# Hybrid decoder step on one core: another table of issue orders, and the first norm's statistics in another PSUM bank

## Chip, cores and metric

The kernel runs on one core of one Trainium2 chip. Its time is the device time in microseconds of one execution. The engines are TensorE (PE, with its weight load PEld), VectorE (DVE), ScalarE (ACT), GpSimd (POOL) and SyncE (SP, which issues the loads and stores). Each takes its instructions strictly in its own program order; an instruction that has to wait holds up everything behind it on that engine.

## What is computed

One layer of a hybrid decoder for 1024 prompt positions and 8 sample sequences of 8 new positions, all in float32. Width 1024, 16 heads of 64 over 4 key and value heads, window 128, FFN width 2816 (two halves), convolution width 3.

```python
def layer(x, ...):
    h = rmsnorm(x, norm_mix)
    q, k, v, gu, gv, ga, gb = split_in(h @ w_in)
    o, nk, nv = attn_prompt(q, k, v, sinks)        # sample rows: attn_sample with cached keys
    vn = layernorm(gelu(gv), ln_g, ln_b)
    s = spatial_gating(gelu(gu), vn, ws, bs)
    merged = sigmoid(ga) * (o @ w_pa) + sigmoid(gb) * (s @ w_pb)
    x = x + merged @ w_out
    f, nconv = conv_ffn(rmsnorm(x, norm_ffn), w_up, conv_w, conv_b, w_down, conv_prev)
    return x + f, nk, nv, nconv, vn
...
y = rmsnorm(x, norm_final)
```

Attention is a softmax over a band of 128 keys with one learned sink per head; `spatial_gating` multiplies by a lower-triangular 128 x 128 matrix per channel group; `conv_ffn` is an up-projection, a causal convolution, `gelu(a) * b` and a down-projection. Outputs are the normed rows and the new caches.

## The kernel before

Activations lie transposed, features on the 128 partitions and tokens along the row. The tokens form two groups: group 0 with 576 columns (64 sample tokens and 512 of the prompt), group 1 with the other 512.

**Precision.** A float32 operand is split into a high part, rounded by a copy (`split` L40, or with a factor L44, both on ACT), and the rest, by a subtraction on DVE (L41). A product is three matmuls: high by high, high by low and low by high. In the code and the trace, `wh` and `wl` are the parts of a weight, `th` and `tl` of a combined activation, `hh` and `hl` of the normed input, `ph` and `pl` of attention's probabilities, `oh` and `ol` of its output.

**Products.** The input projection starts with `gv` from plain products (`mm_tok`, L533), with the weights as `w2h` and `w2l`. Most projections then go through `Chain.product` (L315): seven products of combined quarters in place of eight, in PSUM banks of the pool `psa` named "st", of which there are seven; some results are copied out to SBUF by ACT (`keep`, L294, tiles `k...`). The down-projection does the same in seven rounds (`mm_dn`, L1684; results "dn" added into `x` by L1694).

**The start.** SP loads blocks of `x`, the first block in two pieces (L595 and L602), the others whole (`load_x`, L354), between pieces of the first weights (L157). The products with gv use the input before its norm; the factor 1/rms follows as a scale when a result is read out of PSUM. `stats_tok` sums the squares of one group over the partitions by matmuls with a column of ones (L498), ACT takes the square root (L499, `rst`), DVE the reciprocal, and `gv_out` (L564) reads the gv banks with gelu and that scale.

**The gates.** Sigmoids of the gate columns (L852, tiles `z`) run on ACT beside the last chains of group 1. ACT also splits the sums that SP reads back from memory (`stg` from `sd`, L864, into `s`).

**Attention.** `attention` goes over pairs of (key head, block). For each pair PE makes scores (L1180), ACT exponentials (L1197), DVE the reciprocal of the sum and the scaling (L1199, L1200), PE transposes into `pt` (L1207), ACT and DVE split it to `ph` and `pl`, POOL masks both (L1217, `ch` and `cl`), and PE multiplies by the values (L1231) into the bank `po`, in four matmuls: ph, pl, ch, cl. ACT then copies one half of `po` out (L1236, `ot`), DVE adds the other (L1241, `of`, twice), and the sum is split into `oh` and `ol`. Meanwhile weights of coming products are split on ACT and DVE (`wh<-wraw`, `wl<-wraw,wh`).

**The end.** In the last round of the down-projection ACT squares finished pieces of `x` (L1703, `sq`) and DVE adds the squares up in `acc` (L1706); PE sums them over the partitions into a bank "fs" (L1739, L1729); ACT and DVE make 1/rms of it; `fin_mul` multiplies `x` by it (L1760), part of it on POOL, and SP stores `y`. The first token half is finished so while PE still works on the second.

**The order.** The program is written part by part, and then `issue_order` reorders each engine's whole list by the table `ORDER`: a string of numbers for each engine, each the number of places ahead, in what is left of the written order, from which the next instruction is taken (a dot is 0, "(n)" is n zeros).

```python
        for j in steps + [0] * (len(left) - len(steps)):
            now = left.pop(j)
            if last is not None:
                tc.add_manual_dep(now, last.name, ..., reason="issue order")
```

The order of each engine is thus fixed by the table; waits between engines follow from the data and from the reuse of tiles and banks.

Of the kernel before, what the change touches and what calls it, by code (L numbers as in the profile page):

```python
# [6 lines left out]
F32 = mybir.dt.float32  # L7
# [8 lines left out]
P = 128  # L16
# [18 lines left out]
def layer(tc, a):  # L35
# [11 lines left out]
    with ExitStack() as top:  # L47
# [295 lines left out]
        def pick(x, place, lo, hi):  # L343
# [3 lines left out]
        groups = [dict(g=0, n=576, off=0, soff=NS, base=192, mbase=448, blk0=0,  # L347
                       chunks=[(192, 0, 320), (512, 320, 576)],
                       toks=[("s", 0), *((i, NS + P * i) for i in range(4))]),
                  dict(g=1, n=512, off=576, soff=0, base=0, mbase=0, blk0=4,  # L350
                       chunks=[(0, 0, 512)], toks=[(4 + i, P * i) for i in range(4)])]
# [29 lines left out]
        with ExitStack() as ph1:  # L381
# [106 lines left out]
            psa = pso.enter_context(tc.tile_pool(name="psa", bufs=7, space=PSUM))  # L488

            def bank():  # L490
                return psa.tile([P, 512], F32, name="st")

            def stats_tok(g):

                acc = rsg[g]
                pt = bank()[:, :len(groups[g]["toks"])]
                for i, (_, lo) in enumerate(groups[g]["toks"]):
                    PE.matmul(pt[:, i:i + 1], acc[:, lo:lo + P], ones[:, 0:1], start=True, stop=True)  # L498
                S.activation(rstg[g], pt, AF.Sqrt, bias=eps, scale=1.0 / D)  # L499
                V.reciprocal(rstg[g], rstg[g])  # L500
# [120 lines left out]
            def first_out():  # L621
                stats_tok(0)
                for i in range(len(toks0)):
                    gv_out(0, i, 0, ps5[i])
# [58 lines left out]
            none = lambda: None  # L683
            jobs = [lambda: x_in(0)] + [x for kk in range(4) for x in (t0_job(kk), none)] + [t1_job(kk) for kk in range(4)]
            tokens(1, ("v", 1), lambda i, ps: v_out(1, i, ps), jobs, lambda: stats_tok(1))
            stats_all(1)
            wide["again"] = True
# [650 lines left out]
            for c in range(KD):  # L1338
                for at, go in enumerate(merge(1, c, operand(1))):
                    if at == 1:  # L1340
                        t, u = held.pop(c)
# [317 lines left out]
        with ExitStack() as ph3:  # L1659
# [109 lines left out]
            bank = [psd.tile([P, 512], F32, name="dn") for _ in range(6)]  # L1769
# [90 lines left out]
def issue_order(tc):  # L1860
# [8 lines left out]
    for name, text in ORDER.items():  # L1869
# [15 lines left out]
ORDER = {  # L1885
    "Pool": (
        "(34)mm(23)22..24..6(4)2..24..6(4)2..24..6(4)2..2(8)24..4..4..4..4..4..4..4..4..4..4..4..4(14)ff("
        "4)1..11..1...22(4)2213.2..1(5)6d3..2...3..2...63.b.2...3..2...63..2.8a..3..2..21(4)7.3..2...63.b"
        ".2...3..2...63.b.2...3..2...3.b4.52..2.1...3.4.2.8..3..2...63.b.2...3..2...63.b.2...3..2...6..53"
        "3.2.21"  # L1890
    ),
    "Activation": (
        "1.2(4)b..91.7.1.4..22.1...1(5)223..3(4)1..1.1..1.37..1.3..1..133..1(5)777cc.b..e1e.2.a3.33.22.4."
        ".39.1(5)66a.5..467(4)3.2.1.95a211..7...56(4)3..831.2...351..34(4)2..621.1.363..3.4.b.i4449.33.26"
        ".99.22.11.44..4c..4449e.f3.22.53.268(5)3.4.b.i4449.33.26.993.2.11.44..4c..4449e.f3.22.53.268(5)3"
        ".4.7.a4.39.8.3.2.5.4..9H49.7.d47.73.74.5.7...4.2.33.7b4.7132..62..225.4(4)2274ac2...85237221..2."
        "37.a47.127.6.2.5.4..48..49b7.3.4.5.6...3.4.7.a47.38.74...5.4..48..49b7.3.4.5.6...3.4.6.8d385.2.2"
        "44..2.1.5346246.44..9b.11.53241.3..1..311.y(4)433(5)5(5)2(5)y(5)O4(9)1.1.44(4)1.L(12)1.1.44(4)N1"
        ".44(4)1(9)Q(4)1.1.4(5)1.4(5)1.A(6)1(15)j1.44(5)1..q..H(6)4(5)T44(6)54(6)44(6)5S4(6)54(6)54(6)5P4"
        "(6)54(6)54M(6)54(6)54(6)5r4(6)54(6)54c(5)1...5.61..61.2515.51.123.22.24.15.151.14.51.152.142.24."  # L1900
        "13..45..7..1173..171.111.11(8)11...126.62.24.1..7..1..1.24..1(6)4..44..4.3.9.a.b3..a.922(4)5.4.."
        "9b..bd3...22...46...3.9.a.b3..a.92(5)5.4..9b..bd3...22...46...3.9.a.b3..a.92(5)5.4..9a..9a3...22"
        "421331..b1.3222..11.22..22.8.9bd3...2221571...3.9.a.b3..a.92211..5.4..9b..bd3...22...46...3.9.a."
        "b3..a.92(5)5.4..9b..bd3...22...46...3.9.9.93..7.622...22..51.5225266...5(4)1e.793..a.9322...5.4."
        ".9b..bd3...22...46...3.9.a.b3..a.92(5)5.4..9b..bd3...22...46...3.9.a.b3..a.92(5)5.4..9b..bd3...2"
        "2...46...3.7.7.7h..6..e1..124.341.1111.41525.1(5)1(7)1.1.1.1.1.1.1.1.1..1(4)KK[92]M.[90]L[89]N1M"
        "O[85]O.[83][83].[82][82].1(6)5(4)23.3.3.3.3.3.3.3.3.3.3.3.3.3.3.3.3.3.3.3(9)2j2i4.35e1466a.9.88."
        "71(8)11121..14l13514g62.466aaaaa.91.1.1...1(11)1...1.1...1"
    ),
    "DVE": (  # L1910
        "..nn2(6)91.7.1.4..2.1...1.1(5)23..3(4)1..1.1...26.1.31.2..2f.ee.dd1ck.jj.iii...777cc.bd.c.b2a.93"
        "88.87.62.222(4)2.2.33.22g.1(6)e.e.cccfic(4)8..66a(5)3.5.235f..3.e45..4..468.1.51..3.b.12.23.7.35"
        "..5.1.1...15..35[126]6[125]2[129][129]5.3[132][132]7.g[138].5[135]h.8(4)46(4)2449..26fi(4)66(4)4"
        "47..49.3h.6i.9(5)46(4)2449..26fi(4)66(4)447..47.3d.4e.51..24..254e55555yyyy.4w4v.24dg22.2.1..249"
        "6b.1..22.13c3.d..2..2496b.31..12138.a22..32546.3a.3b.2.13.6274a..47il..58...7.9.e.9.b..1b.ka.9.."
        "1h.7.8(4)6b8d(4)68hk(4)46..6.7.98.7..5.94.3..7.5..14233.32.1.14.2.124723.2.21(4)1(7)L1..227(4)4."
        "..11...11112.1(5)1111...2x(4)22(4)J..11.11..222(4)2N..11(4)2..11.11.252.1.11N.222(4)2..11(4)2R.."
        "11.11.2(4)2.1.2.11.1.2F..112.1.2..11(9)2.1.222...e.11...q(6)F(4)2(4)3332..151M33112.1.222..16154"
        "T1..262143...1..3227..1..332N..151.22..1.4.22O..262.43...1..322..1..332t..262.43(5)4.227g.1.11(4"
        ")1b.22d.11...2.b..34f.2.9.3..714.73.5.b4.66.b.44..587..3..5.1.4.1.3.5...2.2413..31.131.2.3.7..d."  # L1920
        ".35.1..14..2..11.3(8)32(4)u.y(5)25.16.244..3(5)12.2.24143561454223.3...1..114.1.2.41112221.1.1.."
        "2262c5c.ag.9i..7...46(4)2g5g..ddim...aa(4)8..6.f..6..aa.f9i..7...46(4)2g5g..ddim...aa(4)8..6.f.."
        "6..aa.f9i..7...46(4)2g5g..ddhj...aa...8.7..4.4.2.7..5..3.2(5)11.4.e3.cc1h.aaah(4)8..6.f..6..aa.f"
        "9i...6..46(4)2g5g..ddim...aa(4)8..6.f..6..aa.f9i..7...46(4)2g5g..ddim...aa(4)8..6.f..6..aa.e9f.."
        "7...45..3...1b.bag.9..7.6..6.5.2.14.a3ca..7.6ae.5.6(4)25fg..ddim...aa(4)8..6.f..6..aa.f9i..7...4"
        "6(4)2g5g..ddim...aa(4)8..6.f..6..aa.f9i..7...46(4)2g5g..ddim...aa(4)8..6.b..6..66.55...b2a..1133"
        ".33(7)1322.1..7..4..2.1.1(8)1(4)54..1(8)1..11.11.11.11.11...11.a.8..1.4.[75]3(4)11.[67][69].[68]"
        "[70]..11.[65](7)7(6)2b.b.b8..1..6(5)23.3.3.3.3.3.b.b.b8b(5)3(4)23.3.3.3(9)88.7...77.12...11.1..3"
        "..11..11(10)21311111...88(4)4a4...a..118.111.11.111...41.1.2(4)12...2.21.1"
    ),  # L1930
    "SP": (
        "..1(21)6789(4)7...3.2.a.ach(10)7.e.d.3d.c.1o(5)99.aa...948..625(4)33.23f.e..11..1..23(15)271(5)1"
        "(4)11.3..1.OOT1S...TTVV61.1.2..1.13.2..61.1.2..1.13.2..5615...2..232622.12.1212tt.vy..2.424...1."
        ".1.3..62.1.2..464.1.1.4191312.411.21.21c.1512125.1..11.11.1a1411.141...589..1264.11...2231...246"
        "6214..2fs1z1(25)1c.1i6p31...2.m2.63(4)2t.2.s63(4)2.m2.fd.aaab.ib.mf(9)eb(5)79.792(4)3a.d7.6g.j7."
        "1.j1(4)1321(13)1(5)1.2...2.1.21113.52544..4..244..244..54.3.5731.8c4..1133.8K..I2...22..56..y333"
        "..1112.111l11(7)22222211..1.445221.111444455.4477...4455.4477...455.55883(4)3344...44.44...44.66"
        "...1551.44...44.44...44.44...44.99...6(6)1...111f12..3333333..1.98(7)111(40)122.111(5)1.a.9999.8"
        "88l.lmn.no(24)1.1.1...1...1.1.1.1.1.1.1.1"
    ),  # L1940
    "PE": (
        "(26)1(14)1(14)112(3646)8888888(13)999(22)4444(6)9999(405)3(139)3333(31)44(113)4444444(60)4444444"
# [97 lines left out]
```

## Time and profile before

| | before |
|---|---|
| median of three runs | 1503.83 us (1502.03 to 1504.26) |
| profiled execution | 1502.3 us |
| its span in the profile | 1500.6 us |
| mean granted clock of TensorE | 0.998 |
| PE busy | 1487.9 us, 99% |
| DVE, ACT, POOL busy | 79%, 57%, 18% |
| instructions | 30059 |

A row of the timeline reads: start in microseconds from the start of the span, duration, engine, line of the kernel, operation, output and inputs by name, shapes, how many in a row; in brackets the idle time of the engine ahead of it and what ended that. A row of the list of waits reads: engine, tile and line that waited, what it waited for, microseconds in total, how often, the longest. A row of windows gives the stretch, its length, then busy time and number of instructions of PE, weight load, DVE, ACT and POOL, the granted clock, the busy share of the DMA engines and the GB/s moved.

### The profile page before, as it was taken

How to read it: one execution, taken by the hardware profiler on the slowest of the kernel's cores; microseconds unless marked ns; L12 is line 12 of the kernel's file. 1: busy time of each engine (PE TensorE's matmuls, PEld its weight loads, DVE VectorE, ACT ScalarE, POOL GpSimd, SP SyncE). 2: the span in 40 equal slices, each digit the busy share in tenths (PEclk: the TensorE clock that was granted, in tenths of full speed). 3: DMA queues.
4: the chain of work that ended last, by engine and by line, in shares of the span. 5: the costliest groups of instructions: out<-in, count | busy, mean ns of one | idle time of the engine just before them, and what ended most of it. 6: DMA issues, size and time to landing. Idle time of an engine off the chain costs nothing.

```text
span 1500.6 us, 30059 instructions
## 1 busy us (share of the span) xinstructions
PE 1487.9 (99%) x11508; PEld 1451.1 (97%) x11508; DVE 1180.2 (79%) x1886; ACT 856.2 (57%) x1790; POOL 272.4 (18%) x375
## 2 busy tenths in 40 slices
PE   9999999999999999999999999999999999999997
PEld 9999999999998989988989999999999999999997
DVE  7798877655576887979578988898898888785686
ACT  7557676654465776764444555555555556363463
POOL 0001000010030222320234322332142222000002
PEclk9999999999999999999999999999999999999999
DMA  7687546864669757448988433332232216983453
GB/s 258 220 282 249 177 164 224 251 217 158 230 232 306 219 171 236 148 159 303 335 293 283 131 112 119 120 121 109 103 140 101 104 63 231 335 298 98 113 172 142
DMA packets 134431, 289.88 MB, mean 193 GB/s; under 512 B 15760, under 2 KB 36560, under 8 KB 134288
## 3 DMA queue, kind: packets, MB, share of 16 engines
q1 hardware_dynamic: 134144, 287.96, 56.7%
q8 instruction: 90, 1.47, 0.4%
q14 instruction: 53, 0.43, 0.1%
q10 hardware_dynamic: 144, 0.01, 0.0%
HBM read 198.97 MB, written 90.92 MB: 193 GB/s over the span
## 4 chain that ended last, share of the span: by engine, by line
PE 93%; DMA 2%; DVE 2%; ACT 1%; issue 1%; POOL 1%; SPq 0%; POOLq 0%; ACTq 0%; DVEq 0%
PE st L315 50%; PE mm L240 16%; PE dn L1684 14%; PE st L533 7%; PE po L1231 2%; PE sc L1180 2%; PE pt L1207 1%; DMA wl<-upd 1%; PE mx L814 1%; DMA sg1d<-z 0%; DMA x1d<-x1g 0%; DMA x<-xt 0%; POOL cl L1217 0%; DVE pl L41 0%; ACT wh L40 0%
## 5 line engine op out<-in xcount | busy, mean ns | idle before, releaser
L315 PE MATMUL st<-t,wh 128*128 128x288 f32 x2128 | 427.6, 294 | 0.0
L315 PEld LDWEIGHTS st<-t,wh 128*128 128x128 f32 x2128 | 335.5, 188 | 0.1
L315 PE MATMUL st<-t,wl 128*128 128x288 f32 x1064 | 311.9, 293 | 0.0
L315 PE MATMUL st<-th,wh 128*128 128x256 f32 x1064 | 295.2, 278 | 0.6 <-ACT k L294 0.6
L315 PE MATMUL st<-tl,wh 128*128 128x256 f32 x1064 | 294.4, 277 | 0.0
L315 PE MATMUL st<-th,wl 128*128 128x256 f32 x1064 | 294.1, 276 | 0.0
L315 PEld LDWEIGHTS st<-th,wh 128*128 128x128 f32 x1064 | 199.8, 188 | 1.4 <-ACT k L294 1.2
L315 PEld LDWEIGHTS st<-t,wl 128*128 128x128 f32 x1064 | 199.7, 188 | 0.3 <-DMA wl<-upd 0.3
L315 PEld LDWEIGHTS st<-th,wl 128*128 128x128 f32 x1064 | 199.9, 188 | 0.0
L315 PEld LDWEIGHTS st<-tl,wh 128*128 128x128 f32 x1064 | 199.8, 188 | 0.0
L1684 PE MATMUL dn<-th,wh 128*128 128x288 f32 (+1 forms) x616 | 176.7, 287 | 0.1
L1684 PE MATMUL dn<-tl,wh 128*128 128x288 f32 (+1 forms) x616 | 176.5, 286 | 0.0
L1684 PE MATMUL dn<-th,wl 128*128 128x288 f32 (+1 forms) x616 | 175.0, 284 | 0.0
L40 ACT CAST wh<-wraw 128x512 fp32r<-128x512 f32 (+2 forms) x188 | 129.4, 700 | 79.6 <-PE st L315 27.2
L41 DVE TENSOR_TENSOR wl<-wraw,wh 128x512 fp32r<-128x512 f32 (+2 forms) x188 | 148.2, 801 | 31.2 <-ACT wh L40 29.1
L40 ACT CAST wh<-ws 128x512 fp32r<-128x512 f32 x168 | 102.5, 621 | 90.9 <-PE st L315 55.1
L41 DVE TENSOR_TENSOR wl<-ws,wh 128x512 fp32r<-128x512 f32 x168 | 117.6, 711 | 40.9 <-ACT wh L40 40.1
L1684 PEld LDWEIGHTS dn<-th,wh 128*128 128x128 f32 x616 | 115.6, 188 | 0.4 <-ACT zb L341 0.3
L1684 PEld LDWEIGHTS dn<-th,wl 128*128 128x128 f32 x616 | 115.9, 188 | 0.1
L1684 PEld LDWEIGHTS dn<-tl,wh 128*128 128x128 f32 x616 | 115.7, 188 | 0.1
L533 PE MATMUL st<-w2h,hh 128*128 128x256 f32 x288 | 80.2, 279 | 1.0 <-ACT hh L44 0.7
L533 PE MATMUL st<-w2h,hl 128*128 128x256 f32 x288 | 79.8, 278 | 0.0
(281 smaller groups left out, 3181.2 us busy)
## 6 DMA issues: line engine op xcount, KB each, us to landing
wraw<-wt SPq DMA_DIRECT2D x137, 512.0 KB
traw<-td SPq DMA_DIRECT2D x77, 272.0 KB
td<-za SPq DMA_DIRECT2D x22, 544.0 KB
q<-qd SPq DMA_DIRECT2D x16, 512.0 KB
upd<-hl SPq DMA_DIRECT2D x14, 512.0 KB
td<-t SPq DMA_DIRECT2D x11, 544.0 KB
wpart<-wt SPq DMA_DIRECT2D x22, 256.0 KB
qd<-q SPq DMA_DIRECT2D x8, 576.0 KB
```

Of the source, the lines that this page charges most:

```text
L40: S.copy(hi, src)
L41: V.tensor_sub(lo, src, hi.bitcast(F32))
L240: PE.matmul(ps[:, lo:lo + c1 - c0], u[:, k, :], v[:, c0:c1], start=(k == 0 and i == 0), stop=(k == nk - 1 and i == 2))
L315: PE.matmul(ps, u[:, kk, :], v, start=first and kk + i == 0, stop=kk == 3 and i == 2, skip_group_check=True)
L533: PE.matmul(ps, u[:, lo:lo + P], v[:, k, :], start=k + i == 0, stop=k == KD - 1 and i == 2)
L814: PE.matmul(ps[:, P * i:P * i + P], vn[:, i], late["wst"][:, c, :], start=True, stop=True)
L1180: PE.matmul(ps[:, h, o0:256], q, kst[kv][:, e, k0:cur + P], start=e == 0, stop=e == 1)
L1207: PE.transpose(pt[:, h * P:h * P + P], s[:, h, 0:P], ident)
L1231: PE.matmul(po, v[:, kv, :], t, start=e == 0, stop=last)
L1684: PE.matmul(place(m, e), u[:, m, :], v[:, lo:hi], start=new and i + k == 0 and (e == 0 or m % 2 == 0), stop=i == NU - 1 and k == 2, skip_g ...
```

## The change

Two edits. The column that receives the statistics of the first norm comes from the bank "mx" of the same pool instead of one of the seven banks "st":

```diff
             def stats_tok(g):
 
                 acc = rsg[g]
-                pt = bank()[:, :len(groups[g]["toks"])]
+                pt = psa.tile([P, 512], F32, name="mx", bufs=1)[:, :len(groups[g]["toks"])]
                 for i, (_, lo) in enumerate(groups[g]["toks"]):
```

And the strings of `ORDER` for Pool, Activation, DVE and SP are others (PE's stays). The first line of Activation's:

```diff
-        "1.2(4)b..91.7.1.4..22.1...1(5)223..3(4)1..1.1..1.37..1.3..1..133..1(5)777cc.b..e1e.2.a3.33.22.4."
+        "1.2(4)b..91.7.1.4..22.1(9)223..3(4)1..1.1..1.37..1.3..1..133..1(5)777cc.b..e1e.2.a3.33.22.4..39."
```

66 instructions stand some places earlier or later; none is added or removed. Other moves than those below: in SP, L602 now stands ahead of L354 at the start, and loads near 425 us and near the down-projection's start are exchanged; in ACT, a copy (L294) and two sigmoids (L852) stand ahead of splits of `stg` near 425 and 438 us, in the chains of q and k a copy (L294) and casts of q (L834) are exchanged, and in group 0's attention `ot` stands ahead of `ph` three times; in DVE, splits and evacuations of the up-projection between 800 and 850 us are exchanged; in POOL, one run of instructions.

ACT at the first norm, where `rst` is the root of the statistics, `w2h` the high part of a weight and `gv` the gelu of the first results:

```order
 L615 ACTIVATE x_267<-x_267 128x576
-L40 CAST w2h<-wraw 128x1024
+L40 CAST w2h<-wraw 128x1024 x2
 L499 ACT_TABLE_LOAD
-L499 ACTIVATE rst_228<-st,c_eps 128x5
-L40 CAST w2h<-wraw 128x1024
+L499 ACTIVATE rst_228<-mx,c_eps 128x5
 L564 ACT_TABLE_LOAD
 L564 ACTIVATE gv<-st,rst_228 128x256 x4
```

The second split of a weight now stands ahead of the statistics' table load instead of behind its result, and the statistics come from "mx".

DVE in group 1's attention, about 603 to 610 us, before: `nm` is a maximum of scores, `dn` a sum of exponentials, `pl` the low part of the probabilities, `wl` that of a coming weight, `of` and `ol` the output of attention and its low part:

```order
L1241 TENSOR_TENSOR of<-po,ot 64x256
L1194 TENSOR_REDUCE nm<-s 128x4
L1241 TENSOR_TENSOR of<-po,ot 64x256
L41 TENSOR_TENSOR pl<-pt,ph 128x512
L41 TENSOR_TENSOR wl<-wraw,wh 128x1024
L1199 RECIPROCAL dn<-dn 128x4
L41 TENSOR_TENSOR ol_7921<-of,oh_7920 128x2x128
```

And the same place now:

```order
L1241 TENSOR_TENSOR of<-po,ot 64x256
L1194 TENSOR_REDUCE nm<-s 128x4
L41 TENSOR_TENSOR pl<-pt,ph 128x512
L1241 TENSOR_TENSOR of<-po,ot 64x256
L41 TENSOR_TENSOR ol_7921<-of,oh_7920 128x2x128
L41 TENSOR_TENSOR wl<-wraw,wh 128x1024
L1199 RECIPROCAL dn<-dn 128x4
```

The split `pl` stands ahead of the second evacuation, and `of` and `ol` stand between it and the weight's split. In ACT the cast of the same weight stands behind `ph` at this place.

DVE at the end of the down-projection, from about 1478 us: `x_17062` is the second token half, `x_16747` the first, `acc` the sums of squares:

```order
 L1694 TENSOR_TENSOR x_17062<-x_17062,dn 128x288
-L1760 TENSOR_TENSOR x_16747<-x_16747,fs 128x576
+L1706 TENSOR_TENSOR acc_16746<-acc_16746,sq 128x288
+L1694 TENSOR_TENSOR x_17062<-x_17062,dn 128x288
+L1760 TENSOR_TENSOR x_16747<-x_16747,fs 128x576 x2
 L1694 TENSOR_TENSOR x_17062<-x_17062,dn 128x288
 L1706 TENSOR_TENSOR acc_16746<-acc_16746,sq 128x288
-L1760 TENSOR_TENSOR x_16747<-x_16747,fs 128x576
-L1706 TENSOR_TENSOR acc_16746<-acc_16746,sq 128x288
-L1694 TENSOR_TENSOR x_17062<-x_17062,dn 128x288
-L1760 TENSOR_TENSOR x_16747<-x_16747,fs 128x512
```

All three additions into `acc` now stand ahead of the last two scalings of the first half; before, the third addition had three scalings ahead of it.

More of the change, by code (lines that the diff above doesn't have):

```diff
@@ L1887 @@
         "(34)mm(23)22..24..6(4)2..24..6(4)2..24..6(4)2..2(8)24..4..4..4..4..4..4..4..4..4..4..4..4(14)ff("
-        "4)1..11..1...22(4)2213.2..1(5)6d3..2...3..2...63.b.2...3..2...63..2.8a..3..2..21(4)7.3..2...63.b"
-        ".2...3..2...63.b.2...3..2...3.b4.52..2.1...3.4.2.8..3..2...63.b.2...3..2...63.b.2...3..2...6..53"
-        "3.2.21"
+        "4)1..11.2(4)22(4)2213.2..1(5)6d3..2...3..2...63.b.2...3..2...63..2.8a..3..2..21(4)7.3..2...63.b."
+        "2...3..2...63.b.2...3..2...3.b4.52..2.1...3.4.2.8..3..2...63.b.2...3..2...63.b.2...3..2...6..533"
@@ L1891 @@
+        ".2.21"
     ),
     "Activation": (
-        "1.2(4)b..91.7.1.4..22.1...1(5)223..3(4)1..1.1..1.37..1.3..1..133..1(5)777cc.b..e1e.2.a3.33.22.4."
[L1894 to L1907, printed above, removed]
@@ L1908 @@
-        "71(8)11121..14l13514g62.466aaaaa.91.1.1...1(11)1...1.1...1"
+        "1.2(4)b..91.7.1.4..22.1(9)223..3(4)1..1.1..1.37..1.3..1..133..1(5)777cc.b..e1e.2.a3.33.22.4..39."
+        "1(5)66a.5..467(4)3.2.1.95a211..7...56(4)3..831.2...351..34(4)2..621.1.363..3.4.b.i4449.333.6.99("
+        "7)44..4c..4449e.f3.22.53.268(5)3.4.b.i4449.33.26.993.2.11.44..4c..4449e.f3.22.53.268(5)3.4.7.a4."
+        "39.8.3.2.5.4..9H49.7.d47.73.74.5.7...4.2.33.7b4.7132..62..225.4(4)2274ac2...85237221..2.37.a47.1"
@@ new lines @@
+        "27.6.2.5.4..48..49b7.3.4.5.6...3.4.7.a47.38.74...5.4..48..49b7.3.4.5.6...3.4.6.86c37.2.244..2.1."
+        "534624..433.9b.11.53241.3..1..311.y(4)433(5)5(5)2(5)y(5)O4(9)1.1.44(4)1.L(4)1(7)1.1.44(4)N1.44(4"
+        ")1(5)1...Q(4)1.1.4(5)1.4(5)1.A(6)1(5)1(9)j1.44(5)1..q..H(6)4(5)T44(6)54(4)1.44(6)54R(6)54(6)54(6"
+        ")Q54(6)54(6)54M(6)54(6)54(6)s44..1...54(6)54c(5)1...5.61..61.2515.51.123.22.24.15.151.14.51.152."
+        "142.24.13..45..7..1173..171.111.11(8)11...126.62.24.1..7..1(4)24..1(6)4..44...33.9.a.b3..a.9222."
@@ new lines @@
+        "..5.4..9b..bd3...22...46...3.9.a.b3..a.92(5)5.4..9b..bd3...22...46...3.9.a.b3..a.92(5)5.4..9a..9"
+        "a3...22421331..b1.3222..11.22..22.8.9bd3...2221571...3.9.a.b3..a.92211..5.4..9b..bd3...22...46.."
+        ".3.9.a.b3..a.92(5)5.4..9b..bd3...22...46...3.9.9.93..7.622...22..51.5225266...5(4)1e.793..a.9322"
+        "...5.4..9b..bd3...22...46...3.9.a.b3..a.92(5)5.4..9b..bd3...22...46...3.9.a.b3..a.92(5)5.4..9b.."
+        "bd3...22...46...3.7.7.7h..6.f.1..124.341.1111.41525.1(5)1(7)1.1.1.1.1.1.1.1.1..1(4)KK[92]M.[90]L"
@@ L1909 @@
+        "[89]N1MO[85]O.[83][83].[82][82].1(6)5(4)23.3.3.3.3.3.3.3.3.3.3.3.3.3.3.3.3.3.3.3(9)2j2i4.35e1466"
+        "a.9.88.71(8)11121..14l13514g62.466aaaaa.91.1.1...1(11)1...1.1...1"
     ),
@@ L1912 @@
         "88.87.62.222(4)2.2.33.22g.1(6)e.e.cccfic(4)8..66a(5)3.5.235f..3.e45..4..468.1.51..3.b.12.23.7.35"
-        "..5.1.1...15..35[126]6[125]2[129][129]5.3[132][132]7.g[138].5[135]h.8(4)46(4)2449..26fi(4)66(4)4"
+        "..5.1.1...15..35[126]6[125]2[129][129]5.37[131].g.[138]5[136].g8[124](4)46(4)2449..26fi(4)66(4)4"
         "47..49.3h.6i.9(5)46(4)2449..26fi(4)66(4)447..47.3d.4e.51..24..254e55555yyyy.4w4v.24dg22.2.1..249"
@@ L1916 @@
         "1h.7.8(4)6b8d(4)68hk(4)46..6.7.98.7..5.94.3..7.5..14233.32.1.14.2.124723.2.21(4)1(7)L1..227(4)4."
[L1917 to L1929, printed above, removed]
+        "..11...11112.1(5)1111...2x(4)22(4)J..11.11..222..1.2N..11(4)2..11.11.252.1.11N3312121.2..11(4)2R"
@@ new lines @@
+        "..11.11.2(4)2.1.2.11.1.2F..112.1.2.22(10)2.1.222...e.11...q(6)F(4)2(4)3332..151M33112.1333...161"
+        "44.S..262133...1..3227..1..322N..151.32..1.4.22O..262.43...11433...1..222t..262.43(5)4.227g.1.11"
+        "(4)1b.22d.11...2.b..34f.2.9.3..714.73.5.b4.6.5b.44..587..3..5.1.4.1.3.5...2.2413..31.131.2.3.7.."
+        "d..633.1.14..2..11.3.2...11.32..w222.x(4)25.16.244..3(5)12.2.241435616542451221.1..11424163.2444"
+        "313...1..2262c5c.ag.9i..7...46(4)2g5g..ddim...aa(4)8..6.f..6..aa.f9i..7...46(4)2g5g..ddim...aa(4"
@@ new lines @@
+        ")8..6.f..6..aa.f9i..7...46(4)2g5g..ddhj...aa...8.7..4.4.2.7..5..3.2(5)11.4.e3.cc1h.aaah(4)8..6.f"
+        "..6..aa.f9i...6..46(4)2g5g..ddim...aa(4)8..6.f..6..aa.f9i..7...46(4)2g5g..ddim...aa(4)8..6.f..6."
+        ".aa.e9f..7...45..3...1b.bag.9..7.6..6.5.2.14.a3ca..7.6ae.5.6(4)25fg..ddim...aa(4)8..6.f..6..aa.f"
+        "9i..7...46(4)2g5g..ddim...aa(4)8..6.f..6..aa.f9i..7...46(4)2g5g..ddim...aa(4)8..6.b..6..66.55..."
+        "b2a..1133.3.2(6)1322.1..7..4..2.1.1(8)1(4)513.1(8)1..11.11.11.11.11...11.a.8..1.4.[75]3(4)11.[67"
@@ L1930 @@
+        "][69].[68][70]..11.[65](7)7(6)2b.b.b8..1..6(5)23.3.3.3.3.3.b.b.b8b(5)3(4)23.3.3.3(9)88.7...77.12"
+        "...11.1..3..11..11(10)21311111...88(4)4a4...a..118.111.11.111...41.1.2(5)2..3.32..1"
     ),
     "SP": (
-        "..1(21)6789(4)7...3.2.a.ach(10)7.e.d.3d.c.1o(5)99.aa...948..625(4)33.23f.e..11..1..23(15)271(5)1"
-        "(4)11.3..1.OOT1S...TTVV61.1.2..1.13.2..61.1.2..1.13.2..5615...2..232622.12.1212tt.vy..2.424...1."
-        ".1.3..62.1.2..464.1.1.4191312.411.21.21c.1512125.1..11.11.1a1411.141...589..1264.11...2231...246"
@@ L1935 @@
[L1935 to L1939, printed above, removed]
+        "(24)6789(4)7...3.2.a.ach(10)7.e.d.3d.c.1o(5)99.aa...948..625(4)33.23f.e..11..1..23(15)21.5(4)1(4"
@@ new lines @@
+        ")11.3..1.OOT1S...TTVV61.1.2..1.13.2..61.1.2..1.13.2..5615...2..232622.12.1212tt.vy..2.424...1..1"
+        ".3..62.1.2..464.1.1.4191312.411.21.21c.1512125.1..11.11.1a1411.141...589.7.4124..241.231...24662"
+        "14..2fs1z1(25)1c.1i6p31...2.m2.63(4)2t.2.s63(4)2.m2.fd.aaab.ib.mf(9)eb(5)79.792(4)3a.d7.6g.j7.1."
+        "j1(4)1321(13)1(5)1.2...2.1.21113.52544..4..244..244..54.3.5731.8c4..1133.8K..I2...22..56..y333.."
+        "1112.111l11(7)22222211..1.445221.111444455.4477...4455.4477...455.55883(4)3344...44.44...44.66.."
@@ L1940 @@
+        ".1551.44...44.44...44.44...44.99...6(6)1...111f12..3333333..1.988...11122(41)122.111(5)1.a.9999."
+        "888l.lmn.no(24)1.1.1...1...1.1.1.1.1.1.1.1"
     ),
```

## The prediction

> **What bounds the kernel.** I read the page first, then PE's list of waits, then the timeline at each place where that list or PE's spacing shows a hole. Of the page, the busy times and the chain that ended last:
>
> ```profile
> PE 1487.9 (99%) x11508; PEld 1451.1 (97%) x11508; DVE 1180.2 (79%) x1886; ACT 856.2 (57%) x1790; POOL 272.4 (18%) x375
> PE 93%; DMA 2%; DVE 2%; ACT 1%; issue 1%; POOL 1%; SPq 0%; POOLq 0%; ACTq 0%; DVEq 0%
> ```
>
> PE sets the end. The change takes no matmul away, so it can win only where PE stands still. PE's list of waits (microseconds in total, times, longest) names such places:
>
> ```profile
> PE fs L1739 <- DVE acc L1706: 1.5, 1, 1.5
> PE po L1231 <- POOL cl L1217: 1.0, 3, 0.4
> PE st L533 <- ACT hh L44: 0.7, 1, 0.7
> PE st L315 <- ACT k L294: 0.6, 2, 0.4
> PE po L1231 <- ACT s L1197: 0.4, 1, 0.4
> PE st L533 <- ACT rst L499: 0.4, 1, 0.4
> PE po L1123 <- DVE of L1144: 0.3, 1, 0.3
> ```
>
> Moved instructions stand right ahead of all of these but the last. The list counts only recorded idle time; I use the larger number, the distance from one matmul's start to the next less the usual distance, since a matmul's recorded length overlaps its neighbour's.
>
> **Part A, the load of x at 2 us.** SP issues the second half of the first block (L602) behind the whole second block (L354), and the ACT split waits for a load:
>
> ```profile
> 1.74 0.43 SPq L354 DMA_DIRECT2D x<-xt  x1
> 2.21 0.43 SPq L602 DMA_DIRECT2D x<-xt  x1
> 6.43 1.18 ACT L44 ACTIVATE hh<-x,c_gains 128x256 fp32r<-128x256 f32 x2 [1.78 <-DMA x<-xt]
> 6.04 0.28 PE L533 MATMUL st<-w2h,hl 128*128 128x256 f32 x1
> 6.99 0.38 PE L533 MATMUL st<-w2h,hh 128*128 128x256 f32 x1 [0.68 <-ACT hh L44]
> ```
>
> PE stands 6.99 − 6.04 = 0.95 instead of 0.11 (two matmuls of 256 columns in the quoted stretches below start 0.11 apart), so 0.84 at most. The two issues swap. One place earlier in SP is 2.21 − 1.74 = 0.47, and I take that the load lands earlier by as much: 0.45. From 0 (the split is then held by the next load) to 0.84.
>
> **Part B, the first norm at 24 us.** The statistics now lie in the bank "mx", so the next product takes its own "st" bank and no longer the one that ACT still reads:
>
> ```profile
> 23.46 1.17 PE L498 MATMUL st<-c_ones,rs 128*128 128x1 f32 x10
> 24.98 0.39 PE L533 MATMUL st<-w2h,hh 128*128 128x256 f32 x1 [0.36 <-ACT rst L499]
> 24.67 0.27 ACT L499 ACTIVATE rst<-st,c_eps 128x5 f32<-128x5 f32 x1 [1.49 <-PE st L498]
> 24.83 1.04 ACT L40 CAST w2h<-wraw 128x1024 fp32r<-128x1024 f32 x1
> ```
>
> The product starts at 24.98, just when rst ends (24.67 + 0.27 = 24.94); the ten matmuls end at 24.63. So 0.35 of idle time and 0.11 of a slow first matmul (0.39 against 0.28): 0.45, from 0 to that. The same bank change would only move the wait on by one product if the gelu's four instructions came late; ACT's cast of 1.04 now stands ahead of the first table load, in the 1.49 of idle time, so table and gelu come about 1.04 earlier. That is what keeps this term from being given back.
>
> **Part C, the last products of group 1.** ACT copies a partial product (L294) that the next product's accumulation needs; behind it stood other work:
>
> ```profile
> 428.25 0.28 PE L315 MATMUL st<-th,wl 128*128 128x256 f32 x1
> 428.94 0.38 PE L315 MATMUL st<-th,wh 128*128 128x256 f32 x1 [0.42 <-ACT k L294]
> 424.89 0.63 ACT L852 ACTIVATE z<-z 128x512 f32<-128x512 f32 x1
> 425.43 0.39 ACT L341 ACTIVATE z<-st 128x288 f32<-128x288 f32 x1
> 440.11 0.28 PE L315 MATMUL st<-th,wl 128*128 128x256 f32 x1
> 440.58 0.38 PE L315 MATMUL st<-th,wh 128*128 128x256 f32 x1 [0.19 <-ACT k L294]
> 437.75 0.67 ACT L40 CAST s<-stg 128x576 fp32r<-128x576 f32 x1 [1.19 <-DMA stg<-sd]
> ```
>
> The holes are 0.69 − 0.11 = 0.58 and 0.47 − 0.11 = 0.36. In the first, a sigmoid (L852, 425.43 − 424.89 = 0.54 of ACT's time) is moved ahead of a cast that waits for a load anyway, so the copy comes 0.54 earlier. In the second, a copy and a sigmoid move into the 1.19 in which ACT waited for a load. Sum 0.54 + 0.36 = 0.9, from 0 to that. SP issues the loads behind those casts (stg from sd) earlier, and two weight and mask loads later; I cost those at nothing.
>
> **Part D, attention of group 1.** Three times PE waits for the masked low part of the probabilities (POOL, cl), and DVE is what holds POOL:
>
> ```profile
> 609.01 0.40 PE L1231 MATMUL po<-ch,dvst 128*128 128x512 f32 x1
> 609.77 0.50 PE L1231 MATMUL po<-cl,dvst 128*128 128x512 f32 x1 [0.37 <-POOL cl L1217]
> 606.71 0.59 ACT L40 CAST ph<-pt 128x512 fp32r<-128x512 f32 x1
> 607.40 0.69 DVE L41 TENSOR_TENSOR pl<-pt,ph 128x512 fp32r<-128x512 f32 x1 [0.17 <-ACT ph L40]
> 608.01 1.22 DVE L41 TENSOR_TENSOR wl<-wraw,wh 128x1024 fp32r<-128x1024 f32 x1
> 608.16 1.56 POOL L1217 TENSOR_SCALAR_AFFINE_SELECT cl<-pl 128x512 fp32r<-128x512 f32 x1 [0.16 <-DVE pl L41]
> 613.71 0.64 POOL L1217 TENSOR_SCALAR_AFFINE_SELECT cl<-pl 128x512 fp32r<-128x512 f32 x1 [0.29 <-DVE pl L41]
> 605.64 1.05 ACT L40 CAST wh<-wraw 128x1024 fp32r<-128x1024 f32 x1
> ```
>
> Where DVE's long weight split (1.22) follows pl at once, POOL's instruction takes 1.56; where not, 0.64. The list counts 1.0 for the three, one of them here, 0.37; and the matmul behind the wait took 0.50 where the one ahead took 0.40, so 0.1 more each: 1.3. With the 0.4 of the list's row on s (L1197), where an evacuation moves ahead of a split, 1.7. Now ACT makes ph ahead of the weight cast (1.05 earlier at the first place), pl stands ahead of one evacuation, and an evacuation stands between pl and the weight split. The first and the last of these each exceed the wait, so I take all of it, 1.7, and 0 as the other end. What speaks against full value is how full DVE is there (engine columns PE, weight load, DVE, ACT, POOL):
>
> ```profile
> 600.00:650.00 50.00, 48.62 (x345) 45.28 (x344) 47.32 (x89) 39.67 (x125) 17.89 (x30) 1.00 0.41 134
> ```
>
> DVE is busy for 47.32 of 50. What is late next is an evacuation (of), now behind a pl of 0.69, and by the list one has been late only once, for 0.3, in the sample group's part (L1123). In group 0's attention ot goes ahead of ph three times; I cost that at nothing, since the list shows no such wait above 0.3.
>
> **Part E, the end of the down-projection.** PE's longest hole is the wait for the sums of squares of one token half:
>
> ```profile
> 1482.95 0.28 PE L1684 MATMUL dn<-th,wh 128*128 128x256 f32 x1
> 1484.72 0.75 PE L1739 MATMUL fs<-acc,c_ones 128*128 128x288 f32 x2 [1.49 <-DVE acc L1706]
> 1479.54 0.82 DVE L1706 TENSOR_TENSOR acc<-acc,sq 128x288 f32<-128x288 f32 x1
> 1480.94 1.02 DVE L1706 TENSOR_TENSOR acc<-acc,sq 128x288 f32<-128x288 f32 x1
> 1483.22 1.45 DVE L1706 TENSOR_TENSOR acc<-acc,sq 128x288 f32<-128x288 f32 x1
> 1478.61 5.74 POOL L1760 TENSOR_TENSOR x<-x,rb 128x576 f32<-128x576 f32 x4 [219.17 <-ACT rb L1753]
> ```
>
> The hole is 1.77, less 0.11: 1.66. Three sums stand among four scalings (L1760); now two scalings follow the second addition, and the third and fourth come last. POOL's four instructions of 5.74 / 4 = 1.43 end at about 1480.05, 1481.48, 1482.91 and 1484.35, and the sums end 0.31, 0.48 and 0.32 behind three of these: while POOL works, a sum of two SBUF tiles gets through only between two of its instructions. Worked in the new order, the first sum ends before POOL begins, the second at about 1481.95 and the third, without a scaling ahead of it, behind the boundary at 1482.91, at about 1483.35. PE would then start at 1483.40 instead of 1484.72: 1.3. From 0 (the third sum misses its gap) to 1.66. The Trainium skill, "SBUF — State Buffer", sections "SBUF: two separate sides" and "Who interferes with whom", states this as an exclusive lock: a VectorE instruction with two inputs in SBUF and a GpSimd instruction that reads SBUF share a port pair, and the one that starts first keeps it for its whole length. By that rule POOL's fourth instruction, if it starts first, keeps the third sum out until 1484.35, and this part brings nothing; the trace's 1.56 against 0.64, and its sums' ends, agree with a lock.
>
> **Small moves at nothing.** DVE's reordered splits and evacuations around 800 to 850 us, SP's order near 425 and 1260 us, and POOL's small change each pass instructions nobody waits for in the list. For the chance that one such move opens a wait I take off one wait of the smallest size listed, 0.3.
>
> **Sum.** 0.45 + 0.45 + 0.9 + 1.7 + 1.3 − 0.3 = 4.5. The profiled execution took 1502.3 (span 1500.6 and 1.7 around it), so 1497.8 for such an execution. The median of the runs, 1503.83, lies 1.5 above it; the forecast for the median is 1503.83 − 4.5 = 1499.3. With every upper end and no new wait the gain is 0.84 + 0.45 + 0.9 + 1.7 + 1.66 = 5.55, so 1498.3; and the three runs of before lie between 1502.03 and 1504.26, 1.1 to either side of their middle, so 1497.2 at the lowest.
>
> **Rivals.**
>
> *Locked at the end.* The third sum misses its gap, Part E brings 0: gain 3.2, 1500.6. For it: 0.4 us decide, and 1483.22 + 1.45 shows how it looks when the gap is missed. Against: without the scaling the sum is queued before the gap. Chance 0.12.
>
> *Covered.* In Parts C and D the queues are full and the moved work only exchanges one wait for another: 0.45 + 0.45 + 1.3 − 0.3 = 1.9, 1501.9, no measurable change. For it: DVE's 47.32 of 50, and ACT's 39.67. Against: the waiting instruction has spare time behind it where the list is silent. That the bank change does nothing belongs here too: if "mx" were not free at 24 us the product would wait as before, 0.45 of this sum. Chance 0.21.
>
> *The evacuation becomes late, slower.* In attention, ot moves behind wh at two places (1.05 each, and 0.59 of ph at one) and of moves behind pl at five (0.69 each): 2 × 1.05 + 0.59 + 5 × 0.69 = 6.1, and three splits of group 0 behind ot, 3 × 0.59 = 1.8. If each of these is felt in full by the next user of the bank po, 7.9 is lost, A, B, C and E give 2.8 back: 1503.83 + 5.1 = 1508.9. It decides once PE asks for the bank less than 0.69 after DVE now frees it. For it: the one wait on s and one on of are of that kind. Against: every other round shows none. Chance 0.09.
>
> **Numbers.** The forecast case has 0.58, with its own range of 1498.3 to 1500.6. A run of this kernel tells about 0.2%, 3.0 us, from no change. Forecast and "locked" gain more than 3.0: 0.70; "covered" is within: 0.21; the last is slower: 0.09. The range leaves out the last case alone: from 1497.2 to the covered case with the same scatter of 1.1 above it, 1503.0.
>
> **What would show it.** Right: PE's wait for acc at L1739 below 0.3, the waits on cl, k and rst gone, the first hh 0.4 earlier. Wrong, step by step: the third sum still longer than 1 us (E); a wait of po for of or ot in place of cl (D); a wait on k of the old size (C); the first product behind the statistics at 24.9 still, or the same wait one product on (B). A longer median distance of matmul starts would mean that the time is not in the waits at all.

## The result and the profile after

| | before | changed |
|---|---|---|
| median of nine runs | 1503.85 us | 1499.56 us |
| lowest and highest | 1501.85, 1507.28 | 1497.27, 1501.68 |
| profiled execution, its span | 1502.3, 1500.6 | 1497.75, 1496.0 |

The ratio is 0.9971, 95% interval 0.9960 to 0.9983: 4.3 us faster, 4.5 forecast. PE's list of waits in the changed kernel, to be read against the one of before:

```profile
PE st L588 <- DVE c_ones L67: 1.2, 1, 1.2
PE st L1488 <- DVE nacc L1365: 0.8, 1, 0.8
PE sc L1087 <- DVE z L337: 0.6, 1, 0.6
PE fs L1729 <- DVE rt L1721: 0.6, 1, 0.6
PE po L1123 <- DVE of L1144: 0.3, 1, 0.3
PE st L533 <- DVE hl L45: 0.2, 1, 0.2
```

The waits on acc, cl, k, hh, rst and s are gone. One new row stands second: 0.8 at L1488, the statistics of the second norm, where the prediction named no place.

PE executes the same list in both kernels, so the start of the n-th matmul in one trace less its start in the other shows where time goes. From this difference, against the terms of the sum:

| place | forecast | changed less before | what the experiments make of it |
|---|---|---|---|
| A, start to 23 us | -0.45 | -0.32 | not to be told from the scatter of the start |
| B, first norm | -0.45 | -0.53 | needs both edits |
| C, 428 to 443 us | -0.9 | -1.37 | -1.37 by ACT's moves alone |
| 443 to 600 us | | -0.10 | PE's pace and a wait on z, in other kernels too |
| D, attention of group 1 | -1.7 | -1.43 | 0.8 to 1.0 from the change; the rest is a wait that comes and goes |
| second norm, 780 to 815 us | +0.3, for all small moves | +1.23 (1.01 in the wait at L1488) | POOL's and DVE's order ahead of it |
| 815 to 1478 us | | -0.58 | 0.36 of it at 1259 us, in every kernel made from the changed one too |
| E, end | -1.3 | -1.45 | -1.45 alone |

The sum is -4.55: so much earlier PE starts the first of its last eight products (L1729), and the end of the span is 4.56 earlier. (Within the eight another 0.6 is won, but they start 0.21 apart in this one trace of before and 0.11 to 0.12 apart in all others, also where nothing near the end is changed; the end of the span does not follow.) Around the places, the rows that answer to those of before: the first product behind the statistics, the copies in C, the three masked halves (group by line, durations in ns as minimum, median, maximum), and the end.

```profile
23.14 1.17 PE L498 MATMUL mx<-c_ones,rs 128*128 128x1 f32 x10
24.17 0.36 PE L533 MATMUL st<-w2h,hh 128*128 128x256 f32 x1
25.93 1.57 ACT L564 ACTIVATE gv<-st,rst 128x256 f32<-128x256 f32 x4
427.40 0.28 PE L315 MATMUL st<-th,wl 128*128 128x256 f32 x1
427.57 0.39 PE L315 MATMUL st<-th,wh 128*128 128x256 f32 x1
...
L1217 POOL TENSOR_SCALAR_AFFINE_SELECT cl<-pl x28: 634/635/758, 494.4 to 658.7; 128x512 fp32r<-128x512 f32 x28
...
1477.24 1.41 DVE L1706 TENSOR_TENSOR acc<-acc,sq 128x288 f32<-128x288 f32 x1
1478.93 1.18 DVE L1706 TENSOR_TENSOR acc<-acc,sq 128x288 f32<-128x288 f32 x1
1475.51 5.74 POOL L1760 TENSOR_TENSOR x<-x,rb 128x576 f32<-128x576 f32 x4 [218.70 <-ACT rb L1753]
1479.85 0.28 PE L1684 MATMUL dn<-th,wh 128*128 128x256 f32 x1
1480.16 0.75 PE L1739 MATMUL fs<-acc,c_ones 128*128 128x288 f32 x2
```

No cl takes more than 0.76 now; three took 1.56. At the end PE stands 0.31 where it stood 1.77. The two sums beside POOL are still long, 1.41 and 1.18, and end 0.27 and 0.29 behind the ends of POOL's second and third instruction (1475.51 plus two and three times 1.435): they have to wait as before, but early enough.

### The profile page after: what moved, and what is told of

Read it like the earlier page. It is cut to its first block, busy times and chain, and to the rows that moved or that the text cites. A ratio compares the mean times of both kernels' runs of the same rounds, so it can differ in the third digit from the quotient of the medians.

```text
span 1496.0 us, 30061 instructions
## 1 busy us (share of the span) xinstructions
PE 1485.8 (99%) x11508; PEld 1450.2 (97%) x11508; DVE 1181.7 (79%) x1886; ACT 856.9 (57%) x1790; POOL 274.3 (18%) x375
## 4 chain that ended last, share of the span: by engine, by line
PE 96%; DVE 2%; DMA 1%; issue 1%; ACT 0%; POOL 0%; POOLq 0%; SPq 0%; DVEq 0%; ACTq 0%
PE st L315 51%; PE mm L240 17%; PE dn L1684 15%; PE st L533 7%; PE sc L1180 2%; PE po L1231 2%; PE pt L1207 1%; PE mx L814 1%; DMA sg0d<-z 0%; DVE wl L41 0%; DMA x<-xt 0%; DVE ws L176 0%; POOL x L1760 0%; DVE s L41 0%; PE st L510 0%
```

## The experiments

Differences of matmul starts are meant wherever PE is said to be earlier or later.

**The end, two ways.** First, only the end of DVE's table is changed.

```diff
-L1760 TENSOR_TENSOR x_16747<-x_16747,fs 128x576
+L1706 TENSOR_TENSOR acc_16746<-acc_16746,sq 128x288
+L1694 TENSOR_TENSOR x_17062<-x_17062,dn 128x288
+L1760 TENSOR_TENSOR x_16747<-x_16747,fs 128x576 x2
...
```

> The kernel before with only the end of DVE's table changed (three sums ahead of the last two scalings). My theory: nothing moves before 1478 us, the hole ahead of L1739 falls from 1.77 to about 0.3, and the span by 1.5 to 1.8. Rival (the third sum misses the gap between two POOL instructions): the hole stays above 1.2.

PE's hole falls to 0.32, and PE is 1.45 earlier behind it. The span, 1502.0, does not show it and missed the expectation, since PE lost 3.3 between 1260 and 1448 us (last section). Second, DVE's order stays and POOL is cut short; this kernel leaves the other columns unscaled.

```diff
             def fin_mul(th, e, by, cs, eng=V):
...
                     x2 = x1[c // 4, th, e][:, c % 4:c % 4 + 2]
-                    eng.tensor_mul(x2, x2, by[:, None, :].to_broadcast([P, 2, w]))
+                    if eng is G:
+                        x2, by = x2[:, :, 0:32], by[:, 0:32]
+                    eng.tensor_mul(x2, x2, by[:, None, :].to_broadcast([P, 2, x2.shape[2]]))
```

> The kernel before, with POOL's multiplications at the end cut to 32 of 288 columns (the other columns are left unscaled). Theory of a lock by POOL: the three sums (0.82, 1.02, 1.45 before) take about 0.46 each although DVE's order is that of before, and the hole ahead of L1739 falls from 1.77 to below 0.4. Rival, the order alone (sums stand behind scalings, and are long for another reason): the sums keep 0.8 to 1.4 and the hole stays above 1.0.

DVE's and POOL's rows at the end:

```profile
1479.92 0.45 DVE L1706 TENSOR_TENSOR acc<-acc,sq 128x288 f32<-128x288 f32 x1
1480.95 0.45 DVE L1706 TENSOR_TENSOR acc<-acc,sq 128x288 f32<-128x288 f32 x1
1482.65 0.45 DVE L1706 TENSOR_TENSOR acc<-acc,sq 128x288 f32<-128x288 f32 x1
1478.98 0.60 POOL L1762 TENSOR_TENSOR x<-x,rb 128x64 f32<-128x64 f32 x2 [219.84 <-ACT rb L1753]
```

In the same order as before, the sums of 0.82, 1.02 and 1.45 take 0.45 each, the wait on acc leaves the list, and PE is 1.65 earlier at L1739. So POOL made the sums long, and the order of before put them where POOL worked. This is the lock that the prediction took from the trace and that the Trainium skill states ("SBUF — State Buffer", section "Who interferes with whom"); its unfavourable use, a third sum shut out until POOL is done, did not occur.

**The first norm, its two halves apart.** The bank without the orders, and the orders without the bank:

```diff
-                pt = bank()[:, :len(groups[g]["toks"])]
+                pt = psa.tile([P, 512], F32, name="mx", bufs=1)[:, :len(groups[g]["toks"])]
```

> The kernel before with the bank edit alone; all four tables as before. My theory: the product behind the statistics starts at about 24.4 us instead of 24.98, but gelu still starts at about 27.2 and frees the first gv bank at 27.6, and the next product wants it at about 27.1: PE then waits there for about 0.5, so the shift against before is back to 0 to -0.1 by 30 us. Rival: the bank is all of it; no wait at 27 us, and a shift of -0.5 remains from there on.

PE's row behind the statistics, and the one a product later, with gelu on ACT:

```profile
24.48 0.36 PE L533 MATMUL st<-w2h,hh 128*128 128x256 f32 x1
27.17 1.57 ACT L564 ACTIVATE gv<-st,rst 128x256 f32<-128x256 f32 x4
27.70 0.38 PE L533 MATMUL st<-w2h,hh 128*128 128x256 f32 x1 [0.24 <-ACT gv L564]
```

0.53 is won at 24 us and 0.51 of it is lost at 27.7 and one matmul on, where the next product waits for gelu: 0.02 is left. The reverse, where the line above is put back in the changed kernel:

> The changed kernel with the statistics back in one of the seven banks; all tables as changed. My theory: PE waits again for rst, 0.4 to 0.6 at 24 us, and the rest is as in the changed kernel, so a span longer by about 0.5. Rival: the earlier table load alone removes the wait, and the hole stays below 0.2.

```profile
23.58 1.17 PE L498 MATMUL st<-c_ones,rs 128*128 128x1 f32 x10
25.11 0.39 PE L533 MATMUL st<-w2h,hh 128*128 128x256 f32 x1 [0.36 <-ACT rst L499]
```

The wait is back, and none of the 0.53 that the changed kernel wins here is left. So each half alone brings nothing. In this profile PE also waits less for z at 453 us (L1087) than in the changed kernel's, and is 0.6 better off there; but a second profile of the changed kernel (further down) has no such wait either, so that is a difference between executions and gives nothing back. The span, 1497.8, is 1.7 longer, about 1.6 of it for another reason (last section).

**Start and projections.** SP's first exchange and ACT's moves at 425 and 438 us, without SP's other moves:

```diff
+L852 ACTIVATE z_5519<-z_5519 128x512
 L40 CAST s_5962<-stg 128x576
...
+L294 COPY k_6005<-st 128x256
+L852 ACTIVATE z_5807<-z_5807 128x512
 L40 CAST s_6095<-stg 128x576
...
+L602 DMA x_260<-xt 128x256
 L354 DMA x_261<-xt 128x576
-L602 DMA x_260<-xt 128x256
```

> The kernel before with two parts alone: ACT's moves at 425 and 438 us without SP's there, and SP's exchange of the two loads at 2 us. My theory: the holes at 428 and 440 us (0.58 and 0.36 above the usual distance) close, 0.7 to 0.95 in all, since the copies no longer stand behind sigmoids and a split that waits; and the start gains 0.3 to 0.5 by 10 us. Rival, the loads decide: without SP's exchange the split that waits only moves, and less than 0.4 is gained at 425 to 442 us.

0.39 at the start; 0.52, 0.29, 0.46 and 0.10 between 428 and 443 us, 1.37 in all. ACT alone does it; SP's loads there are not needed. The forecast term of 0.9 left out the holes at 438.75 and 442.

The 0.39 at the start is not shown to be the exchange's. It does bring the split forward: the second piece's hh starts at 5.3 to 6.0 us in the eight profiles with the exchange and at 6.4 to 6.6 in the six without. But the matmul that starts at 23.10 us in the kernel before starts at 22.60 to 23.28 in the eight and at 22.72 to 23.23 in the six. By then what is won does not stand out of the scatter.

**Attention, its two halves apart.** DVE's moves alone (ACT as before):

```diff
+L41 TENSOR_TENSOR pl<-pt,ph 128x512
 L1241 TENSOR_TENSOR of<-po,ot 64x256
+L41 TENSOR_TENSOR ol_7921<-of,oh_7920 128x2x128
...
```

> The kernel before with only DVE's moves in group 1's attention. My theory, DVE's long weight split is what holds POOL: cl takes 0.6 to 0.7 at the three places instead of 1.56, PE's waits on cl are gone or below 0.2, and PE is 1.2 to 2.0 earlier by 660 us than at 600. Rival, ph comes too late from ACT: pl waits for ph now, the evacuation behind it is late too, and less than 0.8 is gained.

The group of masked halves, DVE's split at the first place, and PE at the third:

```profile
L1217 POOL TENSOR_SCALAR_AFFINE_SELECT cl<-pl x28: 634/635/756, 497.0 to 662.4; 128x512 fp32r<-128x512 f32 x28
...
606.94 0.69 DVE L41 TENSOR_TENSOR pl<-pt,ph 128x512 fp32r<-128x512 f32 x1 [0.60 <-ACT ph L40]
...
647.82 0.47 PE L1231 MATMUL po<-ph,vst 128*128 128x512 f32 x1 [0.32 <-ACT s L1197]
```

POOL's instruction is short and PE no longer waits for cl, as my theory had it. The gain is not there: DVE now waits 0.60 for ph, PE waits elsewhere, and between 604 and 655 us PE loses 0.35 in all. The rival was right on the sum. ACT's moves alone:

```diff
+L40 CAST ph<-pt 128x512
 L40 CAST wh<-wraw 128x1024
-L40 CAST ph<-pt 128x512
...
+L40 CAST wh<-wraw 128x1024
 L1236 COPY ot<-po 64x512
```

> The kernel before with only ACT's moves in group 1's attention. My theory: pl had waited for ph for only 0.17, so an earlier ph brings pl forward by little, cl is still 1.56 behind the weight split, and the gain between 600 and 660 us is below 0.6. Rival, ph is the bound: the waits on cl vanish and 1.2 to 2.0 is gained.

```profile
607.21 1.56 POOL L1217 TENSOR_SCALAR_AFFINE_SELECT cl<-pl 128x512 fp32r<-128x512 f32 x1 [0.47 <-DVE pl L41]
...
648.87 0.50 PE L1231 MATMUL po<-cl,dvst 128*128 128x512 f32 x1 [0.89 <-POOL cl L1217]
```

cl stays at 1.56, and at the third place the later ot holds an evacuation ahead of pl, so the wait grows from 0.40 to 0.89: PE loses 0.84 between 604 and 650 us. Then both halves together, taken out of the changed kernel:

> The changed kernel with ACT's and DVE's moves in group 1's attention put back. My theory, these are worth about 1 in all, since 1.6 of waits on cl is won and 0.6 is lost again in waits of 0.1 to 0.3 on pl, ot and of: between 595 and 660 us PE falls behind the changed kernel by 0.7 to 1.3. Rival, the prediction's sum: by 1.5 to 1.9. Rival, covered: by less than 0.4.

The three waits on cl are back (1.0 in the list), and PE falls 1.0 behind between 467 and 655 us. So the moves are worth 0.8 to 1.0, and only as a pair. In the changed kernel the three waits give 1.8, counted with the slow matmul behind each; delays of 0.36, 0.34 and 0.23 at 614, 629 and 654 us (by the clock of before), where PE's weight load now waits 0.3 to 0.4 for s or cl, take about half of it back. The remaining 0.6 of the table's 1.43 is the wait on s at 603.89. In the kernels with only the bank, the end or POOL changed, PE is about 0.5 earlier at that same matmul, with nothing moved there; in the one with start and projections changed the wait is there as before. So it comes and goes between executions. No profile of a kernel with moves here has it; whether the moves keep it away stays open.

**The new wait at L1488.** In the changed kernel, DVE comes late to the last addition of squares (L1365):

```profile
791.09 2.93 POOL L275 TENSOR_TENSOR t<-x,x 128x288 f32<-128x288 f32 x1 [3.92 <-DVE x L1424]
801.01 1.40 POOL L1369 TENSOR_TENSOR nacc<-nacc,stg 128x512 f32<-128x512 f32 x1 [3.27 <-ACT stg L1368]
801.18 1.78 DVE L176 TENSOR_TENSOR ws<-wraw 128x512 f32<-128x512 f32 x1
803.55 0.68 DVE L1365 TENSOR_TENSOR nacc<-nacc,traw 128x512 f32<-128x512 f32 x1
```

The weight sum (L176), which meets POOL's addition here, takes 1.78; in the kernel before it took 0.68. First, DVE's last piece ahead of L1365 is put back in the changed kernel.

```diff
+L41 TENSOR_TENSOR t_10269<-x_10339,t_10269 128x288
+L41 TENSOR_TENSOR t_10269<-x_10340,t_10269 128x2x288
 L176 TENSOR_TENSOR ws<-wraw 128x512
...
 L1358 TENSOR_TENSOR x1g_10115<-stg,mm 128x512
-L41 TENSOR_TENSOR t_10269<-x_10339,t_10269 128x288
-L176 TENSOR_TENSOR ws<-wraw 128x512
-L41 TENSOR_TENSOR t_10269<-x_10340,t_10269 128x2x288
 L1365 TENSOR_TENSOR nacc<-nacc,traw 128x512
```

> The changed kernel with one piece of DVE's table put back, seven instructions at 800 us: the weight sum and two splits stand ahead of the second norm's last residual sums again, and the last addition of squares (L1365) follows those sums at once. My theory, this piece made PE's new wait of 0.85 at L1488: the hole of 1.14 falls below 0.3 and all behind it comes 0.8 to 1.0 earlier. Rival, POOL's or ACT's new order is the cause: the hole stays above 0.7.

My theory fell: PE still waits 1.0, and loses 0.44 more than in the changed kernel, 0.16 at this wait and 0.27 just ahead of it. The stretch ahead shows why: POOL and DVE hold each other up.

```profile
795.55 2.21 DVE L41 TENSOR_TENSOR t<-x,t 128x288 fp32r<-128x288 f32 x2
803.01 0.69 DVE L1365 TENSOR_TENSOR nacc<-nacc,traw 128x512 f32<-128x512 f32 x1 [1.58 <-POOL nacc L1369]
790.14 2.93 POOL L275 TENSOR_TENSOR t<-x,x 128x288 f32<-128x288 f32 x1 [3.91 <-DVE x L1424]
801.69 1.29 POOL L1369 TENSOR_TENSOR nacc<-nacc,stg 128x512 f32<-128x512 f32 x1 [4.92 <-ACT stg L1368]
```

Two splits that take 1.11 together in the kernel before take 2.21, and a subtraction of POOL takes 2.93 for 1.73. So POOL's exchange alone was put back, then all of the stretch:

```diff
-L1369 TENSOR_TENSOR nacc<-nacc,stg 128x512
+L1369 TENSOR_TENSOR nacc<-nacc,stg 128x512 x2
 L275 TENSOR_TENSOR t_10385<-x_10340,x_10339 128x288
-L1369 TENSOR_TENSOR nacc<-nacc,stg 128x512
```

> The changed kernel with POOL's one exchange at 790 us put back (the subtraction L275 stands behind the second sum of squares again), DVE as changed. Theory, POOL's exchange alone: the hole ahead of L1488 falls from 1.14 to below 0.4 and PE is 0.7 or more earlier behind it. Rival, DVE's other moves at 780 to 800 us count as much (POOL and DVE then still meet in other pairs): the hole stays above 0.7.

```profile
794.79 0.47 PE L240 MATMUL mm<-mh,wh 128*128 128x512 f32 x1 [0.45 <-DVE x1g L1358]
803.60 0.99 PE L1488 MATMUL st<-c_ones,nacc 128*128 128x1 f32 x8
```

The hole at L1488 closes, but a new one of 0.69 opens 9 us earlier, where DVE's residual sum comes late, so about 0.35 is left. Neither theory holds: the exchange decides this wait, and DVE's pieces decide what it costs elsewhere. Then all is put back: POOL's exchange and five pieces of DVE, which by the trace begin at 771 us. One of the five is shown above and another is this:

```diff
-L41 TENSOR_TENSOR t_10264<-x_10284,t_10264 128x288
 L277 SCALAR_TENSOR_TENSOR t_10332<-t_10332,x_10285 128x288
 L1358 TENSOR_TENSOR x1g_10112<-stg,mm 128x512
+L41 TENSOR_TENSOR t_10264<-x_10284,t_10264 128x288
```

> The changed kernel with the whole stretch of the second norm put back: POOL's exchange and five pieces of DVE's table between 785 and 805 us. Theory, the wait at L1488 comes from these and from nothing earlier: the hole falls below 0.3 as in the kernel before, PE is 0.8 to 1.0 earlier behind it, and the time is about 0.9 below the changed kernel's, 5 below the kernel before. Rival, the stretch is late because PE comes to it 3.7 earlier than a load that keeps its time: the hole stays above 0.7 and the time is that of the changed kernel.

```profile
788.05 1.12 DVE L41 TENSOR_TENSOR t<-x,t 128x288 fp32r<-128x288 f32 x2
791.97 1.72 POOL L275 TENSOR_TENSOR t<-x,x 128x288 f32<-128x288 f32 x1 [0.37 <-DVE x L1424]
802.53 0.69 DVE L1365 TENSOR_TENSOR nacc<-nacc,traw 128x512 f32<-128x512 f32 x1 [1.05 <-POOL nacc L1369]
803.64 0.29 PE L315 MATMUL st<-t,wl 128*128 128x288 f32 x1
803.77 0.95 PE L1488 MATMUL st<-c_ones,nacc 128*128 128x1 f32 x8
```

No hole, and PE is 1.2 earlier behind the stretch than in the changed kernel. Timed beside it on the same chip:

> The changed kernel once more, timed beside the others on the same chip. Every theory: about 4 below the kernel before, and a PE that waits 0.8 to 1.0 at L1488.

| | median | ratio to before, 95% |
|---|---|---|
| before, 11 runs | 1504.21 us | |
| changed, 5 runs | 1500.43 us | 0.9968 (0.9955 to 0.9981) |
| changed, second norm put back, 6 runs | 1497.18 us | 0.9952 (0.9938 to 0.9966) |

The last has the lowest median. Its interval overlaps that of the changed kernel, so the timing alone does not separate them; the trace does, by the 1.2 at one place. The 3.25 between the two medians is more than that, and the two profiled executions, with spans of 1495.8 for the last and 1495.1 for the changed kernel, do not show it at all: they differ by as much elsewhere.

## Why the prediction was right

The forecast of 1499.3 met 1499.56, with the main waits named rightly, but with terms of which D was too large, C and E too small, and the small moves far off.

- **A** had the mechanism right, since the split starts earlier. Its size is not shown: -0.32 in this pair of profiles lies within the scatter of the start.
- **B** held in size and in mechanism: the bank alone moves the wait on by one product, as written.
- **C** was mis-sized: 0.9 for 1.37, since only the two quoted holes were counted.
- **D** had the mechanism for cl right (1.56 to 0.64). Two steps failed. "The first and the last of these each exceed the wait" credits ACT's earlier ph by itself, but alone it loses 0.84, and the delays that the new order makes were put at nothing, though they take back about half of what the waits on cl give. And the 0.4 of the wait on s cannot be credited to the change. 0.8 to 1.0 is left of 1.7. The third rival, the late evacuation, is real in the half kernels, far below its price of 7.9.
- **The small moves at nothing** were the costliest step: they were priced at 0.3 in all, and those at the second norm alone cost 1.2. The prediction looked for waits in PE's list of before, and a place without a row there was taken for safe. The meeting of DVE and POOL that it used for D and E was at work there, against the change. This term, and the list of moves ahead of it, also leave out DVE's moves from 771 to 800 us and near 1255 and 1288 us. The last two stand at places where the change gains. At 1259 us PE is about 0.36 earlier in all seven profiles of the changed kernel and the kernels made from it, and in none of the other seven. And at 1291 us PE loses 0.6 to 1.4 in a wait for DVE's evacuation (L1694) in four of those other seven and in none of the first, where that evacuation and a weight's load ahead of it come earlier. The profile of before is not one of the four, so the table above does not show it. No kernel changed these two places alone.
- **E** was 0.15 too small, with the third sum passing between two instructions of POOL as worked out.

The sum was thus good partly by luck: C, E, B and the places without a term gave 1.4 more than forecast, D and A 0.4 less in this pair, and the second norm cost 0.9 more than was put by. The two profiled executions are also only one of each kernel; both lie 1.5 to 1.8 below their medians.

## What to carry to other kernels

A move of one instruction can turn on which pair of VectorE and GpSimd instructions meets: before moving either, look for two-input instructions of VectorE beside GpSimd's, also where nobody waits yet. Moves on two engines that feed each other (ph on ACT, pl on DVE; bank and table load) should be tried as pairs and halves, since a half may lose what the pair gains. Compare the start of the same matmul in two traces, and check with other executions, and with a kernel that changed nothing at that place, whether a difference there is the change's: waits of 0.5 to 1 us came and went here between executions (at 453, 604 and 1291 us).

## What the hardware showed besides

**Two paces of PE.** In three of the twelve experiments' profiles (the end alone, DVE's attention alone, POOL's exchange) matmuls of 256 columns started 117.7 ns apart from about 1256 to 1446 us, against 113.3 in the others, at a granted clock of 1.00. Windows of the changed kernel and, second, of the one with only the end changed:

```profile
1320.00:1370.00 50.00, 50.00 (x410) 50.00 (x409) 35.92 (x65) 26.29 (x50) 0.00 (x0) 1.00 0.62 191
...
```

```profile
1320.00:1370.00 50.00, 50.00 (x402) 50.00 (x402) 37.55 (x69) 27.37 (x54) 0.00 (x0) 1.00 0.66 206
```

402 matmuls in place of 410, both without a gap; 3.3 us over the stretch. The nine runs of the changed kernel differ by 4.4 us; whether the pace makes much of this is not shown, since only single executions were profiled. In the three profiles the slow pace begins at 1254 to 1259 us and ends at 1444 to 1448, each time behind a gap of 0.2 to 0.4 between two matmuls, which the other kernels have too. What sets it stays open.

**A short drop of the clock.** In the two profiles with the orders alone and with attention undone, the granted clock was 0.51 and 0.62 from 806 to 809 us, right behind the wait at L1488, and PE lost about 1.6 there; in two profiles of the changed kernel with the same wait, and in the one with DVE's piece put back, where it is longer, the clock was 1.00. The first of them:

```profile
806.00:809.00 3.00, 3.00 (x16) 3.00 (x15) 0.10 (x1) 0.41 (x1) 0.00 (x0) 0.51 0.95 325
```

16 matmuls in place of 26. Whether the wait brings the drop was not tried.
